# A hybrid decoder layer on one core: fourth quarter copied by ScalarE, branch stages one step later, left sums on GpSimd, scores over 128 rows, spatial products pinned

## The chip, the cores and the metric

The kernel runs on one core of a Trainium2 chip. The metric is the device time of the whole program in microseconds, the median of three runs. A profiled execution of the same program gives the rows of the trace. TensorE has its matmuls (PE) and its weight loads (PEld) in rows of their own; DVE is VectorE, ACT is ScalarE, POOL is GpSimd, SP is SyncE, which here issues most of the DMAs.

## The reference

One decoder layer on 2048 tokens of width 1024. The normalised input is projected once, by a matrix of 9992 columns, into four branches of width 512 and the logits of four gates:

```python
h = _rmsnorm(x, norm_pre)
cols = h @ w_in
y_a = _deltanet_branch(dn_qkv, dn_z, dn_b, dn_a, conv_w, a_log, dt_bias, dn_norm)
y_b = _spatial_gating_branch(gm_uv, gm_z, gm_norm, spatial_w, spatial_b)
y_c = _sliding_window_branch(sw_q, sw_k, sw_v, sw_z, sinks)
y_m = _memory_branch(xm_q, xm_z, mem_kv)
proj = jnp.einsum("btnc,ncd->btnd", ys, w_up)
merged = jnp.sum(gates * proj, axis=2)
return x + _rmsnorm(merged @ w_out, norm_post)
```

Branch A is a gated delta rule in chunks, with a short causal convolution on its inputs and a triangular solve per chunk. Branch B mixes 128 positions per channel group by a causal matrix. Branch C is attention over a window of 128 tokens with 8 query heads on 2 key heads of 64 channels. Branch M attends to 256 memory tokens.

## The kernel before

**Tiling.** The tokens are worked off in four passes of 512 (`TB`). Values are kept in float32 and split into a high and a low part of the matmul type (`hi`, `lo`, lines 234 to 248), so that each product is three matmuls (`mac3`, lines 271 to 273). ScalarE casts the high part of a weight tile (line 243), VectorE or GpSimd subtracts for the low one (line 244).

**Quads.** In the first pass a projection of 256 columns (`proj2`) is done directly, and sums of weight tiles are formed on GpSimd (line 362) and kept in device memory. In the other three passes each projection is a `quad`: a scheme with seven products in place of eight on halves of the 1024 input channels and of the 512 tokens. Its four output quarters C11, C12, C21 and C22 lie in two PSUM banks, C11 and C21 in the first, C12 and C22 in the second. Between the products ScalarE and VectorE copy and add quarters: line 315 copies C11 to C12 after the first product, line 318 keeps C21 as `p7` after the second, lines 321 and 322 add C12 to C21 after the third, and line 324 makes C22 from C12 and `p7` after the fifth. The last two products then end the first and second bank. Two quads run alternately (`job`), one some steps ahead of the other. Each pass has 37 of them. Three of the products take sums and differences of the input's quarters as left factors, which `left_sums` makes at the head of a pass (lines 465 to 484), from the same input tiles that the next `branch_b_v` reads.

**The order of the work.** Everything is written as Python generators. One generator is in the foreground (`fg`); each time that it yields, `step` advances every background generator by one. So a `yield` in a side branch says how many steps of the foreground's products lie before its next instructions in the program text. A scheduler then orders each engine's instructions by a model of their times, near to the text's order but not bound to it; `tc.keep_in_program_order` binds an instruction behind the one that stands before it on its engine. On the chip each engine takes its instructions strictly in the resulting order.

**The places touched.**
- The constants' rows (`crow`, lines 182 to 187) come by DMA from ScalarE's and GpSimd's queues, after the first eight loads of x on SyncE's (line 89).
- `dn_gates` makes the decay logits `g`, waits nine steps, and then does three cumulative products (`gps`, lines 687 to 689).
- `dn_step` solves the triangular systems on VectorE in 32 pairs of instructions (lines 839 and 840) with a scratch tile `pr`, sends the solution through device memory (line 852), waits four steps and goes on with the products of line 862.
- `normalize` (line 943) squares the scan's output on ScalarE one step after the scan made it.
- `mix` in `branch_b` does the four spatial products of a channel group (line 1014), and its output is split (`ysplit`, line 560 on ScalarE) three steps later.
- `branch_c_kv` keeps the keys' high part twice: for each of the two key heads `kph` has the head's 64 channels in its own half of the rows, and a copy in the other half, where the queries hold their low part. The low part `kpl` is one tile, with each head's 64 channels in its own half.
- `block` in `branch_c` does the scores of 128 queries and 256 keys: per pair of query heads and key head one product over all 128 rows (line 1117) and one over the 64 rows of the head with `kpl` (line 1120). A step after the row maxima come the exponentials (line 1138).
- `part` in `branch_m` likewise has exponentials one step behind the maxima (line 1213).

## Time and profile before

| | us |
|---|---|
| median of three runs | 2882.06 |
| lowest and highest | 2878.23, 2888.78 |
| the profiled execution | 2874.15 |
| its span, first to last instruction | 2872.4 |
| TensorE busy | 2683.5 (93%) |
| VectorE busy | 1937.6 (67%) |
| ScalarE busy | 1395.2 (49%) |
| GpSimd busy | 975.8 (34%) |

The busy time of an engine is the union of its instructions' times over the span. A row of the timeline gives start, duration, engine, line, operation, tiles, shape and count, and in brackets the idle time of that engine just before it with what ended it. A row of waits gives an engine's instruction, whom it waited for, the total, how many times, and the longest.

### The profile page before, as it was taken

The page shows a single profiled execution, that of the slowest core. Times are in us where ns is not written, and L with a number is a line of the kernel's source. Part 1 is how long each engine was busy: PE and PEld are TensorE (multiplying, and loading weights), DVE is VectorE, ACT ScalarE, POOL GpSimd, SP SyncE. Part 2 cuts the span into 40 slices and gives each one's busy share as a digit, 9 for nine tenths or more (in the row PEclk, how much of TensorE's full clock was granted, in tenths as well). Part 3 has the DMA queues.
Part 4 walks back from the last instruction along what each step waited for, and adds up shares of the span by engine and source line. Part 5 has one row for each costly group of instructions (what it writes and reads, how often), then busy time and mean ns, then how long its engine had stood idle before and what let it go on. Part 6 is the DMA issues. An engine that isn't in the chain of part 4 may idle for free. (4 is left out here: it accounts for less than half of the span.)

```text
span 2872.4 us, 49476 instructions
## 1 busy us (share of the span) xinstructions
PE 2683.5 (93%) x17457; PEld 2350.7 (82%) x17457; DVE 1937.6 (67%) x3914; ACT 1395.2 (49%) x3116; POOL 975.8 (34%) x848
## 2 busy tenths in 40 slices
PE   7989998999989999999999899999998989998998
PEld 5867777888788888889879888888987988887987
DVE  7576687555676768766568676786556876777654
ACT  4434342433475455355456446545455644644543
POOL 3524444354236443101223634310124363421011
PEclk9999999999999999999999999999999999999999
DMA  5364544455356354445635535444553553553553
GB/s 173 113 182 147 165 136 136 120 167 191 119 136 164 109 132 134 121 114 139 196 99 147 157 98 138 138 119 122 147 180 112 150 148 96 151 142 89 148 151 121
DMA packets 465791, 398.22 MB, mean 139 GB/s; under 512 B 101440, under 2 KB 360584, under 8 KB 465544
## 3 DMA queue, kind: packets, MB, share of 16 engines
q1 hardware_dynamic: 444056, 356.23, 45.0%
q10 hardware_dynamic: 21392, 38.84, 3.7%
q8 instruction: 137, 2.24, 0.3%
q14 instruction: 110, 0.90, 0.1%
q0 software_dynamic: 96, 0.01, 0.0%
HBM read 338.60 MB, written 50.86 MB: 136 GB/s over the span
## 5 line engine op out<-in xcount | busy, mean ns | idle before, releaser
L599 POOL TENSOR_TENSOR merged<-merged,gt 128x512 f32<-128x512 f32 x96 | 141.0, 1471 | 657.4 <-DVE gt L598 630.7
L362 POOL TENSOR_TENSOR T<-raw 128x512 f32<-128x512 f32 x74 | 103.5, 1408 | 98.6 <-DMA raw<-in_w_in_dram 68.4
L839 DVE TENSOR_TENSOR pr<-L,U 128x8 f32<-128x8 f32 (+31 forms) x256 | 111.6, 436 | 23.9 <-DMA L<-scr 18.6
L244 DVE TENSOR_TENSOR gate3lo<-raw,gate3hi 128x512 fp32r<-128x512 f32 x100 | 73.0, 733 | 66.8 <-ACT gate3hi L243 66.0
L244 POOL TENSOR_TENSOR gate1lo<-raw,gate1hi 128x512 fp32r<-128x512 f32 x69 | 88.0, 1290 | 79.0 <-ACT gate1hi L243 65.0
L244 DVE TENSOR_TENSOR gate0lo<-raw,gate0hi 128x512 fp32r<-128x512 f32 x100 | 77.8, 781 | 53.9 <-ACT gate0hi L243 53.2
L243 ACT CAST gate2hi<-raw 128x512 fp32r<-128x512 f32 x100 | 61.8, 621 | 104.8 <-PE gate L272 63.8
L243 ACT CAST gate1hi<-raw 128x512 fp32r<-128x512 f32 x100 | 61.0, 618 | 104.8 <-PE gate L272 45.3
L362 POOL TENSOR_TENSOR T<-raw,T 128x512 f32<-128x512 f32 x74 | 105.4, 1425 | 15.1 <-issue 6.8
L271 PE MATMUL wo<-wohi,mh 128*128 128x512 f32 x256 | 102.6, 401 | 6.3 <-DVE gt L598 6.3
L271 PE MATMUL gate<-hhi,gate1hi 128*128 128x256 f32 (+1 forms) x256 | 86.6, 338 | 20.3 <-DVE gate L322 20.3
L243 ACT CAST gate3hi<-raw 128x512 fp32r<-128x512 f32 x100 | 61.7, 621 | 90.4 <-PE gate L272 46.4
L243 ACT CAST gate0hi<-raw 128x512 fp32r<-128x512 f32 x100 | 62.0, 620 | 85.7 <-PE gate L272 48.2
L273 PE MATMUL wo<-wohi,ml 128*128 128x512 f32 x256 | 100.1, 391 | 0.0
L272 PE MATMUL wo<-wolo,mh 128*128 128x512 f32 x256 | 99.7, 389 | 0.0
L271 PE MATMUL gate<-hhi,gate2hi 128*128 128x256 f32 (+1 forms) x256 | 83.8, 327 | 11.4 <-DVE gate L322 11.4
L244 DVE TENSOR_TENSOR gate2lo<-raw,gate2hi 128x512 fp32r<-128x512 f32 x100 | 73.8, 739 | 27.2 <-ACT gate2hi L243 26.9
L952 POOL TENSOR_TENSOR or<-ov,mhalf 128x2 f32<-128x2 f32 x32 | 23.4, 730 | 190.4 <-DVE ov L950 190.4
L598 DVE SCALAR_TENSOR_TENSOR gt<-gt,up 128x512 f32<-128x512 f32 x96 | 65.0, 681 | 29.1 <-PE up L273 28.5
L273 PE MATMUL gate<-hhi,gate1lo 128*128 128x256 f32 (+1 forms) x256 | 83.8, 330 | 0.4 <-POOL gate1lo L244 0.4
L272 PE MATMUL gate<-hlo,gate1hi 128*128 128x256 f32 (+1 forms) x256 | 83.8, 327 | 0.0
L271 PE MATMUL gate<-hhi,gate0hi 128*128 128x256 f32 (+1 forms) x256 | 80.7, 315 | 2.7 <-ACT u L321 2.1
(644 smaller groups left out, 11036.9 us busy)
## 6 DMA issues: line engine op xcount, KB each, us to landing
raw<-in_w_in_dram SPq DMA_DIRECT2D x461, 256.0 KB, 3.1
raw<-tsum SPq DMA_DIRECT2D x444, 256.0 KB, 2.9
tsum<-T ACTq DMA_DIRECT2D x148, 256.0 KB, 3.7
raw<-in_w_up_dram SPq DMA_DIRECT2D x96, 256.0 KB, 2.9
raw<-in_w_out_dram SPq DMA_DIRECT2D x64, 256.0 KB, 3.1
raw<-in_w_in_dram SPq DMA_DIRECT2D x104, 128.0 KB, 2.9
xx<-in_x_dram SPq DMA_DIRECT2D x32, 256.0 KB, 5.3
raw<-in_w_up_dram SPq DMA_DIRECT2D x64, 128.0 KB, 3.0
```

Source lines behind the costliest of these rows:

```text
L243: A.copy(hi, raw)
L244: ins = eng.tensor_tensor(lo, raw, hi.bitcast(F32), op=ALU.subtract)
L271: ins = T.matmul(ps, lh, rh, start=first, stop=False, skip_group_check=more)
L272: T.matmul(ps, lh, rl, start=False, stop=False, skip_group_check=more)
L273: T.matmul(ps, ll, rh, start=False, stop=last, skip_group_check=more)
L362: G.tensor_tensor(raw[n], raw[u], raw[v], op=ALU.subtract)
L598: V.scalar_tensor_tensor(t, t, 1.0, ps, op0=ALU.add, op1=ALU.mult)
L599: G.tensor_tensor(merged[:, d], merged[:, d], t, op=ALU.add)
L839: V.tensor_tensor(pv, L[:, i, i:32].unsqueeze(1).broadcast_to([P, 8, n]), U[:, :, i:32], op=ALU.mult)
L952: G.tensor_tensor(r, v, mhalf[:, :2], op=ALU.pow)
```

## The change

- The rows of constants are loaded by SyncE, ahead of the rows of x.
- In a quad ScalarE copies C12 to C22 after the fifth product, and VectorE adds `p7` in place.
- All four left sums of a half are made on GpSimd; before, two of them were VectorE's.
- The low part of the keys gets a tile for each key head, with zeros in the other head's rows, cleared by GpSimd at the start of `branch_c_kv`. The score products with it run over all 128 rows, and each follows its high partner at once.
- The cumulative products of the decay gates come after 14 steps in place of nine in the last three passes; the first solve's result is used after eight steps in place of four; the scan's norm, the split of the mixed output, and the exponentials of the window and the memory attention come one step later.
- The first of a group's spatial products is bound to its place in the text.
- The solve's scratch comes from the ring `e` of six buffers, once for the whole solve.

```diff
--- before.py
+++ after.py
@@ -91,2 +91,8 @@
 
+    crow = tmp("crow")[0:69, 0:P]
+    nc.sync.dma_start(crow[0:8], norm_pre[0].rearrange("(k p) -> k p", p=P))
+    nc.sync.dma_start(crow[8:56], conv_w[0].rearrange("j (c p) -> (j c) p", p=P))
+    nc.sync.dma_start(crow[56:64], norm_mem[0].rearrange("(k p) -> k p", p=P))
+    nc.sync.dma_start(crow[64:68], gm_norm[0].rearrange("(k p) -> k p", p=P))
+    nc.sync.dma_start(crow[68:69], dn_norm[0].rearrange("(k p) -> k p", p=P))
     first_rows = [load_rows(x[t * P:(t + 1) * P], "x", dtmp) for t in range(NB)]
@@ -181,8 +187,2 @@
 
-    crow = tmp("crow")[0:69, 0:P]
-    nc.scalar.dma_start(crow[0:8], norm_pre[0].rearrange("(k p) -> k p", p=P))
-    nc.scalar.dma_start(crow[8:56], conv_w[0].rearrange("j (c p) -> (j c) p", p=P))
-    G.dma_start(crow[56:64], norm_mem[0].rearrange("(k p) -> k p", p=P))
-    G.dma_start(crow[64:68], gm_norm[0].rearrange("(k p) -> k p", p=P))
-    G.dma_start(crow[68:69], dn_norm[0].rearrange("(k p) -> k p", p=P))
     ccol = cp.tile([P, 69], F32, name="ccol")
@@ -229,3 +229,3 @@
 
-    nsplit, solving, fast = [0], [], []
+    nsplit, solving, solved, fast = [0], [], [], []
     ON_DVE = ("gu", "gv", "gz", "az", "xq", "xz", "gate0", "gate2", "gate3", "u0", "u2", "u3", "wo")
@@ -323,3 +323,4 @@
             elif i == 4:
-                V.tensor_tensor(ps["C22"], ps["C12"], p7, op=ALU.add)
+                A.copy(ps["C22"], ps["C12"])
+                V.tensor_tensor(ps["C22"], ps["C22"], p7, op=ALU.add)
             elif i >= 5:
@@ -471,3 +472,3 @@
                 a[n] = tmp("s1") if n == "A22" else ctmp("sa")
-                (G if n in ("A22", "A12") else V).tensor_tensor(r3(a[n], 2), h.bitcast(F32)[:, js], l.bitcast(F32)[:, js], op=ALU.add)
+                G.tensor_tensor(r3(a[n], 2), h.bitcast(F32)[:, js], l.bitcast(F32)[:, js], op=ALU.add)
             V.tensor_tensor(a["A22"], a["A21"], a["A22"], op=ALU.add)
@@ -495,3 +496,3 @@
         return (tp.tile([P, 2 * (P + TB)], F32R, name=f"{nm}h", tag="cma", bufs=1),
-                tp.tile([P, H * MEM], F32R, name=f"{nm}l", tag="cmb", bufs=1),
+                tp.tile([P, 2 * (P + TB)], F32R, name=f"{nm}l", tag="cmb", bufs=1),
                 tp.tile([P, 2 * W], F32, name=f"{nm}v", tag="cmv", bufs=1))
@@ -500,3 +501,3 @@
         h, l, v = cm
-        return (h[:, :H * MEM].rearrange("p (h m) -> p h m", h=H), l.rearrange("p (h m) -> p h m", h=H),
+        return (h[:, :H * MEM].rearrange("p (h m) -> p h m", h=H), l[:, :H * MEM].rearrange("p (h m) -> p h m", h=H),
                 v.rearrange("p (a c) -> p a c", a=2))
@@ -682,4 +683,3 @@
                         nexpa.unsqueeze(1).broadcast_to([P, NB, H]), op=ALU.mult)
-        for _ in range(9):
-            yield
+        yield from wait(14 if fast else 9)
         gps = dnp("gps")
@@ -834,5 +834,5 @@
         work = 0
+        pr = etmp("pr")
         for i in range(31, -1, -1):
             n = 32 - i
-            pr = tp.tile([P, 256], F32, name="pr", tag="pr", bufs=1)
             pv = pr[:, :8 * n].rearrange("p (a b) -> p a b", a=8)
@@ -852,3 +852,4 @@
         nc.sync.dma_start(ltv, scu.rearrange("a b j i -> (b j) a i"))
-        yield from wait(4)
+        yield from wait(4 if solved else 8)
+        solved.append(q)
 
@@ -943,3 +944,3 @@
             def normalize(c=c, o=o):
-                yield
+                yield from wait(2)
                 ss = small("oss", 2)
@@ -1013,3 +1014,5 @@
                     for c in range(NB):
-                        T.matmul(sps[:, c * P:(c + 1) * P], vs[c][:, g * P:(g + 1) * P], wsT[:, g], start=True, stop=True)
+                        ins = T.matmul(sps[:, c * P:(c + 1) * P], vs[c][:, g * P:(g + 1) * P], wsT[:, g], start=True, stop=True)
+                        if c == 0:
+                            tc.keep_in_program_order(ins)
                     s = tmp("gs")
@@ -1023,2 +1026,3 @@
                     yield
+                    yield
                     ys.append(ysplit(s, "yb"))
@@ -1032,3 +1036,4 @@
     def branch_c_kv(p):
-        kp2, kpl, vtt = cm_tiles("kp")
+        kp2, kpl2, vtt = cm_tiles("kp")
+        kpl = kpl2.rearrange("p (a b) -> p a b", a=2)
         kph = kp2.rearrange("p (a b) -> p a b", a=2)
@@ -1038,3 +1043,6 @@
             V.tensor_copy(kph[rs, a, 0:P], kch.bitcast(F32)[rs])
-        V.tensor_copy(kpl[:, 0:P], kcl.bitcast(F32))
+        for a in range(2):
+            rs, ro = slice(a * 64, (a + 1) * 64), slice(64 - a * 64, 128 - a * 64)
+            G.tensor_copy(kpl[ro, a], zero[ro].broadcast_to([64, P + TB]))
+            V.tensor_copy(kpl[rs, a, 0:P], kcl.bitcast(F32)[rs])
         V.tensor_copy(vt[:, 0], vc)
@@ -1046,5 +1054,5 @@
                     A.copy(kph[rs, a, P:], ps[rs])
-                    V.tensor_tensor(kpl[rs, P:P + TB], ps[rs], kph.bitcast(F32)[rs, a, P:], op=ALU.subtract)
+                    V.tensor_tensor(kpl[rs, a, P:], ps[rs], kph.bitcast(F32)[rs, a, P:], op=ALU.subtract)
+                    V.tensor_copy(kcl[rs], kpl.bitcast(F32)[rs, a, TB:TB + P])
                     V.tensor_copy(kch[rs], kph.bitcast(F32)[rs, a, TB:TB + P])
-                V.tensor_copy(kcl, kpl.bitcast(F32)[:, TB:TB + P])
 
@@ -1117,5 +1125,3 @@
                     T.matmul(pss[a][:, i * 256:(i + 1) * 256], qs[i][a][:, bs], kph[:, a, kw], start=True, stop=False)
-                for a in range(2):
-                    rs = slice(a * 64, (a + 1) * 64)
-                    T.matmul(pss[a][:, i * 256:(i + 1) * 256], qs[i][a][rs, bs], kpl[rs, kw], start=False, stop=True)
+                    T.matmul(pss[a][:, i * 256:(i + 1) * 256], qs[i][a][:, bs], kpl[:, a, kw], start=False, stop=True)
             for a in range(2):
@@ -1134,3 +1140,3 @@
             V.tensor_tensor(i2(es_), i2(nm), sv, op=ALU.add)
-            yield
+            yield from wait(2)
             den = small("cden", 4)
@@ -1208,3 +1214,3 @@
             V.tensor_scalar_mul(m, m, -1.0)
-            yield
+            yield from wait(2)
             pr = ctmp("xp")
```

## Rows read from the trace of the kernel before

**Rows 1.** The page: busy time of TensorE, share of the span, instructions.

```profile
PE 2683.5 (93%) x17457; PEld 2350.7 (82%) x17457; DVE 1937.6 (67%) x3914; ACT 1395.2 (49%) x3116; POOL 975.8 (34%) x848
```

**Rows 2.** Waits of TensorE over the whole span: total, times, longest.

```profile
PE gate L271 <- DVE gate L322: 32.3, 15, 4.7
...
PE z L862 <- DMA lt<-scu: 14.1, 5, 6.0
...
PE gps L687 <- DVE g L681: 11.7, 3, 3.9
...
PE xq L271 <- ACT u L321: 8.0, 3, 2.7
...
PE xz L271 <- ACT xz L315: 7.6, 3, 2.5
...
PE sq L271 <- ACT sq L315: 7.3, 6, 2.0
...
PE gv L272 <- DVE gvlo L244: 5.2, 4, 1.5
...
PE gs L1014 <- ACT gv L991: 4.5, 6, 1.2
```

**Rows 3.** Timeline of TensorE: one block of scores, first pass.

```profile
248.45 0.39 PE L1117 MATMUL scp<-kph,sq 128*128 128x256 f32 x2
...
248.78 0.38 PE L1120 MATMUL scp<-kpl,sq 64*128 64x256 f32 x2
...
249.83 0.50 PE L271 MATMUL gate<-hhi,gate1hi 128*128 128x512 f32 x1
```

**Rows 4.** Timeline of TensorE: full products of 256 columns, one behind another.

```profile
1400.00 0.28 PE L272 MATMUL gate<-hlo,gate0hi 128*128 128x256 f32 x1
...
1400.12 0.28 PE L273 MATMUL gate<-hhi,gate0lo 128*128 128x256 f32 x1
```

**Rows 5.** Timeline of ScalarE, third pass: a split and the copy behind it.

```profile
1602.27 0.62 ACT L560 CAST ybh<-gs 128x512 fp32r<-128x512 f32 x1 [3.71 <-DVE gs L1022]
...
1603.32 0.36 ACT L315 COPY sq<-sq 128x256 f32<-128x256 f32 x1
```

**Rows 6.** Timeline of ScalarE, second pass: the tanh and the copy behind it.

```profile
1106.46 0.63 ACT L713 ACTIVATE dnvt<-dnva 128x512 f32<-128x512 f32 x1 [0.60 <-DVE dnva L708]
...
1107.18 0.36 ACT L315 COPY xz<-xz 128x256 f32<-128x256 f32 x1
```

**Rows 7.** Timeline of ScalarE, third pass: the square in the scan's norm.

```profile
1945.63 0.31 ACT L947 ACTIVATE junk<-on 128x128 bf16<-128x128 f32 x1 [2.37 <-DVE on L941]
```

**Rows 8.** Windows: busy time of each engine in ten microseconds, granted clock.

```profile
1500.00:1510.00 10.00, 7.01 (x31) 6.75 (x32) 3.12 (x17) 7.71 (x16) 2.92 (x4) 0.52 0.14 39
```

**Rows 9.** Timeline of TensorE, second pass: second product of a quad.

```profile
1353.71 0.39 PE L271 MATMUL gate<-shi,gate0hi 128*128 128x256 f32 x1 [0.43 <-ACT gate L315]
```

**Rows 10.** Timeline at the head of the third pass: TensorE and ScalarE.

```profile
1505.46 1.22 PE L1014 MATMUL gs<-wsT,gv 128*128 128x128 f32 x4 [0.30 <-ACT gv L991]
...
1505.93 0.36 ACT L315 COPY dn<-dn 128x256 f32<-128x256 f32 x1
...
1506.34 0.56 PE L271 MATMUL dn<-hhi,dn1hi 128*128 128x256 f32 x1
```

**Rows 11.** Timeline of the start: SyncE's loads of x, TensorE.

```profile
0.81 3.74 SPq L89 DMA_DIRECT2D xx<-in_x_dram  x8
...
12.53 0.35 PE L190 MATMUL cps<-ident,crow 69*128 69x69 f32 x1 [7.00 <-DMA crow<-in_conv_w_dram]
...
18.49 2.64 PE L444 MATMUL xtp<-ident,xx 128*128 128x128 f32 x13 [2.13 <-DVE xx L430]
```

**Rows 12.** Timeline at the end of the second pass: VectorE and GpSimd.

```profile
1474.00 1.74 POOL L472 TENSOR_TENSOR sa<-hhi,hlo 128x512 f32<-128x512 f32 x1 [0.27 <-DVE slo L481]
...
1474.50 1.79 DVE L481 TENSOR_TENSOR slo<-sa,shi 128x512 fp32r<-128x512 f32 x1
...
1476.87 1.28 DVE L472 TENSOR_TENSOR sa<-hhi,hlo 128x512 f32<-128x512 f32 x2
```

## The prediction, made before the changed kernel was run

> **What bounds the kernel now.** I read the page's busy times first. TensorE is busy 93% of the span [rows 1], so the time is TensorE's own work plus its idle 7%, about 189 us (2872.4 less 2683.5). A helper engine matters only where TensorE stands for it, or where its work is laid on TensorE. I then read TensorE's waits: they are short and many [rows 2]. VectorE and ScalarE end nearly all of them, and most rows count a multiple of three, because the last three passes repeat one schedule. Last I read timelines around those waits, to see what stood ahead of the late instruction on its own engine. Engines take their queues in order, so a late instruction delays everything behind it. That view decides what "one step later" is worth, since the edit moves an instruction back in a queue and takes no work away.
>
> **Scores at 128 rows.** A block now has four 128-row and four 64-row products of 256 columns, in alternating pairs. The eight take from 248.45 to 249.83, 1.38 us [rows 3]; 22 of the 32 blocks lie within 1.3 to 1.5 us. Products of the same columns on 128 rows throughout start 0.12 us apart [rows 4], so eight would take 0.96. The 64-row pairs thus cost more than full ones, 0.42 us a block, 13.4 us in 32 blocks. A few blocks stand beside waits that keep part of it, so I take **-12**. The Trainium skill (TensorEngine Tiling, Theoretical Speedup) says that a contraction of 64 lets two row tiles run at once, up to twice as fast. By it a pair costs one slot, six slots 0.72 us, and the change loses 0.24 us a block. The same page (Key Properties) says that a change of tiling mode drains the engine; the 1.38 us side with that sentence and against the first.
>
> **Stages one step later.** Three waits per pass have one form: ScalarE stands at an instruction of a side branch, and a copy out of a quarter product (lines 315, 318, 321) that TensorE needs is queued behind it.
> - The split of a gated output stands 3.71 us for VectorE, and the copy for the query projection comes only behind it [rows 5]. TensorE's share is 2.0 us, the longest of its sq row [rows 2], once a pass: 6.0 us.
> - The softmax exponentials and the convolution's tanh stand ahead of the xz copy [rows 6]: 7.6 us in three passes [rows 2].
> - The square of the scan's output stands 2.37 us for VectorE [rows 7], ahead of the copies for xq: 8.0 us [rows 2].
>
> Together 21.6 us. A step later, the copy can go first. I don't take all of it. In the second case the tanh itself had stood 0.60 us for VectorE, and with the exponentials gone it may hold the copy to the same time. In all three the next late thing is a VectorE sum or a weight split. I take half, **-11**, between 0 and -21.6. The clock adds to any such gain. Where TensorE stood long its granted clock fell afterwards: 0.52 in ten microseconds of which it was busy seven [rows 8], near its lower level of 1.2 GHz. I leave that for the range.
>
> **Decay gates five steps later, spatial products pinned.** At the head of each of the last three passes TensorE's queue holds products for the spatial branch that wait for ScalarE (4.5 us) and the cumulative sums that wait for VectorE (11.7 us) [rows 2]. Both edits take these out of the way, 16.2 us if that were the end. It need not be. The second product of the first quad writes the bank which the copy of line 315 reads, and such a product waits for that copy even where nothing else is in the way [rows 9]. Here the copy runs at 1505.93, behind ScalarE's GELUs, squares and scalings, and TensorE resumes at 1506.34 [rows 10]. Unless ScalarE's order changes, the hole stays, and the spatial products leave it for places where TensorE is busy: at 1.2 us or less for four of their records [rows 10], some 2 us a pass. I take **-3**, between -16 and +6.
>
> **First solve.** Its result waits 6.0 us for the DMA that brings the solution back [rows 2]; four more steps of other work cover that, and nothing before the next gate of the pass needs the scan. Only the first solve changes, as its list is never emptied. **-6**.
>
> **Constants by SyncE.** TensorE no longer stands 7.0 us for them, but it then stands for the rows of x anyway and resumes at 18.49 for the last of these [rows 11]. Eight loads take 3.74 us to issue, so five more ahead put the rows 2.3 us later. ScalarE's queue saves two issues, GpSimd's three. **+2**, between -3 and +4.
>
> **Left sums on GpSimd.** Twelve sums of 0.64 us (two in 1.28) leave VectorE, 7.7 us; GpSimd's own sum there takes 1.74. They lie in the stretch in which VectorE is full and TensorE ends up waiting for a split (5.2 us in four waits) [rows 2, 12]. Against it stands the row in which a GpSimd sum runs and a VectorE split beside it takes 1.79 us, where such an instruction takes 0.64 alone [rows 12]: 1.15 us for each of twelve is 14. The Trainium skill (GPSIMD Engine Reference, the SBUF interfaces) says that GpSimd contends with VectorE instructions that have two SBUF inputs, and this row agrees. GpSimd's roots for the last output and splits queue behind the sums too. I take **0**, between -5 and +14.
>
> **Fourth quarter by ScalarE.** The copy comes once a quad, 37 quads a pass by the calls, 111 in all, at 0.36 us [rows 5]: 40 us more on ScalarE, and the VectorE addition stays at its length. Nobody waits for that addition now. The new chain is longer, copy then addition, before the last product writes the same bank. It is covered by the fifth product and, where two quads alternate, by the other quad's products of 12 x 0.12 = 1.44 us each. What costs is a copy that stands in ScalarE's queue ahead of a weight cast or another copy. Bounds: 0 if covered; the sister chain at the third quarter, with a cover of one product less, costs TensorE 32.3 us for the addition and 8.0 for the copy [rows 2], so +40. With the longer cover I take **+4**.
>
> **The rest.** Two GpSimd clears a pass, two small VectorE copies in place of one, and the solve's scratch taken from a ring of six shared buffers. No row shows such a clear; each lies between a short GpSimd instruction and the 1.7 us sum of [rows 12]. Eight of them at most stretch VectorE by 1.15 us: 0 to +9. Scores need the cleared half only several quads later. I take **+1**. The later step of the memory branch's exponentials and the wait in the scan's norm change no total.
>
> **The sum** is -12 -11 -3 -6 +2 +0 +4 +1 = -25. The profiled execution took 2874.15 us, of which the span is 2872.4, so 2849. The median shown is 7.9 us above that execution; I add it: **2857 us**.
>
> **The rivals.**
> - *Everything comes home.* All waits aimed at vanish and no cost shows: -13.4 -21.6 -16.2 -6 -5, -62, and 2820. For it: each edit has a wait of its size. Against: ScalarE's own chain at the head of a pass, and the queues behind each wait. 0.12.
> - *The waits change their name.* The steps and pins gain nothing, as the next instruction in line is as late: -12 -6 +7 = -11, so 2871. For it: VectorE is full in the very stretches where these waits stand. 0.22.
> - *ScalarE becomes the bound, and the kernel slower.* The copies cost the +40 of the sister chain, and the one-step gains, which are ScalarE's own time, are gone: -12 -3 -6 +2 +40 +1 = +22, so 2904. It decides once the copy starts more than the cover, some 2.9 us, after its product. For it: ScalarE stands that long in [rows 5]. Against: half of ScalarE's time is free, and no wait for the present addition is seen. 0.09.
> - *A pair of 64-row products is one slot after all*, the 1.38 us having another cause: +7.7 in place of -12, so 2877. The 0.12 us spacing of full products speaks against it. It is what the Trainium skill's first sentence above would give. 0.03.
>
> **How the numbers follow.** My forecast has 0.54, its own range 2838 to 2872 by the bounds of the steps and sums. Half a percent, 14.4 us, is about what a measurement of this kernel can tell from no change: faster is below 2867.7, slower above 2896.5. Faster holds most of the forecast (0.47), the first rival (0.12) and a third of the second (0.07): 0.66. Slower is the third rival, 0.09. The rest is 0.25. From 2824 to 2886 leaves out the outer part of the first rival and the third.
>
> **What the profile after would show.** Blocks of scores at 0.96 us, 128-row products alone. No TensorE wait for the cumulative sums, nor for copies of line 315 behind a split of an output. The hole at the head of a later pass either still ends at line 315's copy, as I say, or is gone. A wait of the last product of a quad for the added copy or the addition behind it would show the third rival. A longer VectorE split beside GpSimd's sums, with a longer TensorE wait at the end of the gv product, would show the price of the left sums. I am wrong if TensorE's idle falls by much more or less than some 14 us.

## The result, and the profile after

The changed kernel takes **2901.4 us** (median of 13 runs, 2896.0 to 2912.9), the kernel before in the same comparison 2885.8 (2877.0 to 2891.8). The ratio is 1.0065, 95% interval 1.005 to 1.008: slower by 0.65%, some 19 us, where -25 was forecast and the range ended at 2886. In this section and the next a difference in microseconds is the ratio less one, times the median of before in that comparison; the interval is worked out likewise. A profiled execution is one execution, and can lie more than 10 us from its kernel's median, as here: it took 2912.4 us, with a span of 2910.7.

The busy times of the page after, engines in the order of [rows 1]:

```profile
PE 2685.3 (92%) x17457; PEld 2362.4 (81%) x17457; DVE 1930.4 (66%) x3910; ACT 1424.4 (49%) x3227; POOL 995.1 (34%) x865
```

TensorE is as busy as before (2685.3 against 2683.5) and idle for 225 us in place of 189. The rows of TensorE's waits in the changed kernel that answer to [rows 2], or are new or larger beside it (engine, line, whom it waited for, total us, times, longest):

```profile
PE gate L271 <- DVE gate L322: 26.5, 13, 4.7
PE gps L687 <- DVE g L682: 17.0, 3, 5.8
PE z L863 <- DMA lt<-scu: 14.7, 2, 7.9
PE scp L1125 <- DVE szs L1167: 10.1, 7, 3.1
PE gate L271 <- DVE gate L325: 9.2, 6, 1.8
PE gv L272 <- DVE gvlo L244: 9.2, 6, 2.2
PE xq L271 <- ACT u L321: 9.0, 3, 3.0
PE xz L271 <- ACT xz L315: 8.3, 3, 2.8
PE scp L1125 <- DMA sq<-sqlo: 8.0, 5, 2.8
...
PE sq L271 <- ACT sq L315: 7.3, 6, 2.0
PE up L273 <- DVE u2lo L244: 7.0, 9, 1.3
```

The reader is to see three things. The waits at which the steps were aimed are all there: sq for line 315 7.3 us as before, xz for line 315 8.3 (7.6), xq for line 321 9.0 (8.0), gps for g 17.0 (11.7), z for its DMA 14.7 (14.1). Only gs for gv has gone. And four have come or grown by 6 us or more: the gate product for line 325, which is the addition behind the new copy (9.2, none before), up for the split of u2 (7.0, none before), the score product for line 1167, the window's output (10.1, in before 2.6 on its line 1161), and the score product for the load of the query's split (8.0, in before 2.0).

What did come as forecast is the score block, first pass, TensorE's timeline (start, duration, engine, line, operation, tiles, shape):

```profile
252.99 0.36 PE L1125 MATMUL scp<-kph,sq 128*128 128x256 f32 x1
253.19 0.28 PE L1126 MATMUL scp<-kpl,sq 128*128 128x256 f32 x1
253.30 0.28 PE L1125 MATMUL scp<-kph,sq 128*128 128x256 f32 x1
...
254.02 0.40 PE L271 MATMUL gate<-hhi,gate1hi 128*128 128x512 f32 x1
```

From 252.99 to 254.02 it takes 1.03 us for eight products, against 1.38 in [rows 3]; over 32 blocks the products take some 11 us less. The kernel loses some 30 us elsewhere.

### The profile page after: what moved, and what is told of

Read it like the earlier page. It is cut to its first block, busy times and chain, and to the rows that moved or that the text cites. A ratio compares the mean times of both kernels' runs of the same rounds, so it can differ in the third digit from the quotient of the medians.

```text
span 2910.7 us, 49597 instructions
## 1 busy us (share of the span) xinstructions
PE 2685.3 (92%) x17457; PEld 2362.4 (81%) x17457; DVE 1930.4 (66%) x3910; ACT 1424.4 (49%) x3227; POOL 995.1 (34%) x865
## 5 line engine op out<-in xcount | busy, mean ns | idle before, releaser
L839 DVE TENSOR_TENSOR pr<-L,U 128x8 f32<-128x8 f32 (+31 forms) x256 | 114.7, 448 | 21.2 <-DMA L<-scr 15.3
L244 DVE TENSOR_TENSOR gate0lo<-raw,gate0hi 128x512 fp32r<-128x512 f32 x100 | 78.8, 793 | 55.6 <-ACT gate0hi L243 55.5
L1149 POOL TENSOR_TENSOR sc<-sc,cden 128x512 f32<-128x512 f32 x32 | 41.3, 1292 | 153.8 <-DVE cden L1148 106.7
L271 PE MATMUL gate<-hhi,gate3hi 128*128 128x256 f32 (+1 forms) x256 | 84.2, 329 | 0.2
```

The source lines that it names most:

```text
L244: ins = eng.tensor_tensor(lo, raw, hi.bitcast(F32), op=ALU.subtract)
L271: ins = T.matmul(ps, lh, rh, start=first, stop=False, skip_group_check=more)
L839: V.tensor_tensor(pv, L[:, i, i:32].unsqueeze(1).broadcast_to([P, 8, n]), U[:, :, i:32], op=ALU.mult)
L1149: G.tensor_tensor(scv, scv, den.unsqueeze(2).broadcast_to([P, 4, P]), op=ALU.mult)
```

## The experiments

Each kernel below is the kernel before with the edits named, unless it says otherwise. "The other steps" are the first solve, the norm, the output split and the gates.

| kernel | edits | difference, us | 95% |
|---|---|---|---|
| a_scores | scores on 128 rows | -9.5 | -14.1 to -4.6 |
| b_exps | both exponentials later | +12.7 | +7.2 to +18.1 |
| m_expw | the window's exponentials later | +12.7 | +8.1 to +17.3 |
| n_expm | the memory branch's later | +1.7 | -2.9 to +6.3 |
| c_copy | fourth copy by ScalarE | +0.6 | -4.9 to +6.3 |
| d_left | left sums on GpSimd | +7.5 | +2.6 to +12.4 |
| e_rest | the other steps | -8.7 | -14.4 to -2.6 |
| f_pin | pins and gates | +2.0 | -2.3 to +6.3 |
| g_crow | constants by SyncE | -1.2 | -6.6 to +4.3 |
| i_scrc | scores, other steps, constants | -6.9 | -10.9 to -2.9 |
| j_copy | i_scrc and the fourth copy | -1.4 | -6.0 to +3.2 |
| l_pin | i_scrc and the pins | -8.4 | -13.0 to -3.5 |
| h_part | i_scrc, the copy and the pins | -4.0 | -8.4 to +0.6 |
| s_noexpw | changed kernel, window's exponentials as before | +10.7 | +6.0 to +15.6 |
| r_noleft | changed kernel, left sums as before | +17.3 | +11.8 to +22.8 |
| k_bound | output split later, and bound | -6.0 | -12.4 to 0 |
| o_scbound | scores, and that split | -12.7 | -17.8 to -7.5 |
| p_setbound | i_scrc, and that split | **-20.7** | -26.5 to -15.3 |

**The scores alone.**

```diff
-                for a in range(2):
-                    rs = slice(a * 64, (a + 1) * 64)
-                    T.matmul(pss[a][:, i * 256:(i + 1) * 256], qs[i][a][rs, bs], kpl[rs, kw], start=False, stop=True)
+                    T.matmul(pss[a][:, i * 256:(i + 1) * 256], qs[i][a][:, bs], kpl[:, a, kw], start=False, stop=True)
```

> Only the scores on 128 rows (with the two GpSimd clears, the wider buffer and the ring for the solve's scratch). Theory A, the parts of the prediction hold and add: 11 to 13 us faster than before, since the blocks of the changed kernel already measure 0.95 to 1.04 us in place of 1.38. Theory B, the gain in a block is given back at waits of TensorE for VectorE that end at the same time as before, because VectorE has the same work: within 4 us of before, score blocks at 0.96 us all the same, and TensorE's idle larger by what its busy time lost. In the changed kernel TensorE's wait of the scores for the split of the query grew from 2.0 to 8.0 us and that for line 1167's product from 2.6 to 10.1; under B both grow here too, under A neither does.

Ratio 0.9967: -9.5 us, nearer to theory A, with an interval that ends just beyond B's 4 us. TensorE's busy time fell to 2671.7, 11.8 less than before, and neither of the two waits that B named grew: the score products stand 1.5 us for the load of the query's split (2.0 before) and 1.0 for the window's output (2.6). So these two waits of the changed kernel belong to other edits. B's other sign did come: TensorE's idle in this profile is 202.2 us, 13.3 more than before, in many small waits of other products. So a part of the gain may be given back, and -9.5 is not the gain of the blocks alone.

**The later exponentials.**

```diff
-            yield
+            yield from wait(2)
             den = small("cden", 4)
...
-            yield
+            yield from wait(2)
             pr = ctmp("xp")
```

> Only the two later steps of the exponentials (window and memory branch), the one pair of the moved steps that changes much of the order in which the engines' queues are filled. Theory A: no time of its own to 5 us faster, the wait of the xz product for line 315's copy (7.6 us before) shorter. Theory B, a later step moves the branch's other instructions, and what they wait for is as late as ever, in another place: slower by 3 to 12 us, with the xz wait at 7 to 9 us and a longer wait for the first solve or for the memory branch's products.

+12.7, above B's range. The wait of xz for line 315 is 7.5 us: the step didn't take it away. The up product's wait for the split of u2 (6.8 us, nine times) is the changed kernel's. The two edits were then taken apart.

> Only the window's exponentials two steps later. Theory A, these carry the cost of the pair, as they are what reorders more of TensorE's queue and of VectorE's (the window's products of all four quads of a gate): +9 to +14 us, with the up product's wait for its weight split (6.8 us in nine, none before) and the memory branch's products' waits. Theory B, the memory branch's carry it: within 4 us of before.

> Only the memory branch's exponentials two steps later. Theory A, the window's carry the cost: within 4 us of before. Theory B: +9 to +14 us. Under both the wait of the xz product for line 315 stays at 7 to 8 us, since on ScalarE's queue that copy still stands behind the same tanh and casts.

The window's step costs it all, +12.7, the memory branch's +1.7. But m_expw's profile shows that most of this is neither of the waits expected. The score products' groups on TensorE, before and then m_expw (line, shape, count, busy us, mean ns, idle ahead of them):

```profile
L1117 PE MATMUL scp<-kph,sq 128*128 128x256 f32 x128 | 30.8, 313 | 5.3 <-DVE szs L1161 2.6 <-DMA sq<-sqlo 2.0 <-ACT dn L315 0.7
L1120 PE MATMUL scp<-kpl,sq 64*128 64x256 f32 x128 | 24.8, 384 | 0.0
```

```profile
L1117 PE MATMUL scp<-kph,sq 128*128 128x256 f32 x128 | 38.7, 339 | 5.8 <-DVE szs L1161 3.5 <-DMA sq<-sqlo 2.3
L1120 PE MATMUL scp<-kpl,sq 64*128 64x256 f32 x128 | 37.3, 386 | 0.0
```

The 64-row products are busy 37.3 us in place of 24.8, the 128-row ones 38.7 in place of 30.8, with little change of the means. The two groups overlap each other; counted once, TensorE is busy with score products for 66.2 us in place of 49.1, 17 more. One such product isn't longer, but fewer of them overlap. TensorE's timeline of half a block, and its weight loads in the same stretch:

```profile
277.73 0.39 PE L1117 MATMUL scp<-kph,sq 128*128 128x256 f32 x1
278.05 0.38 PE L1120 MATMUL scp<-kpl,sq 64*128 64x256 f32 x1
278.36 0.38 PE L1117 MATMUL scp<-kph,sq 128*128 128x256 f32 x1
278.67 0.38 PE L1120 MATMUL scp<-kpl,sq 64*128 64x256 f32 x1
278.98 0.50 PE L271 MATMUL gate<-hhi,gate1hi 128*128 128x512 f32 x1
```

```profile
278.05 0.18 PEld L1120 LDWEIGHTS scp<-kpl,sq 64*128 64x128 f32 x1
278.36 0.19 PEld L1117 LDWEIGHTS scp<-kph,sq 128*128 128x128 f32 x1
```

In before, TensorE has all 64-row products in pairs, 64 of them, and the two of a pair run at once: a pair takes 0.38 us in [rows 3], and so does the single product here. The later step made the scheduler deal half of them out singly: 32 pairs and 64 singles. Then 64 and 128 rows alternate at every product, each weight load begins only with its own product (278.05 in both), and products start 0.31 us apart. In the changed kernel, where all have 128 rows, they start 0.12 apart, and the load runs ahead: that of the product at 253.19 above is

```profile
253.07 0.19 PEld L1126 LDWEIGHTS scp<-kpl,sq 128*128 128x128 f32 x1
```

So the 12.7 us here is mostly a cost that the scores on 128 rows take away, and can't be added up beside them.

**The copy and the left sums.**

```diff
-                V.tensor_tensor(ps["C22"], ps["C12"], p7, op=ALU.add)
+                A.copy(ps["C22"], ps["C12"])
+                V.tensor_tensor(ps["C22"], ps["C22"], p7, op=ALU.add)
```

> Only the fourth quarter's copy by ScalarE, with VectorE's addition behind it. Theory A, the longer chain is covered: +4 us and no wait on the new addition. Theory B, the third rival on a smaller scale: the waits of the gate product for the new addition that the changed kernel shows (9.2 us in six, none before) come back here, with some more at copies and weight casts that stand behind the new copy on ScalarE: +9 to +20 us.

+0.6, with theory A's +4 inside the interval. TensorE waits for the new addition nowhere in this kernel, so the 9.2 us of the changed kernel need another edit beside the copy. What came with the copy is the score products' wait for the load of the query's split: 6.4 us, 2.0 before and 8.0 in the changed kernel.

```diff
-                (G if n in ("A22", "A12") else V).tensor_tensor(r3(a[n], 2), h.bitcast(F32)[:, js], l.bitcast(F32)[:, js], op=ALU.add)
+                G.tensor_tensor(r3(a[n], 2), h.bitcast(F32)[:, js], l.bitcast(F32)[:, js], op=ALU.add)
```

> Only the left sums on GpSimd. The order of TensorE's and ScalarE's queues is that of before, so this is the clean price of the move. Theory A: 0, with the wait at the end of the gv product (5.2 us in four) no longer than before. Theory B, GpSimd's sums take longer and lie in front of what TensorE needs, or lengthen VectorE's splits beside them: the gv wait at 8 to 10 us, as in the changed kernel (9.2), and +3 to +14 us.

+7.5, theory B, with a wait of gv for its split of 9.9 us. GpSimd's and VectorE's timelines at the head of the third pass:

```profile
1483.25 1.74 POOL L472 TENSOR_TENSOR sa<-hhi,hlo 128x512 f32<-128x512 f32 x1 [0.34 <-DVE finv L416]
...
1485.92 1.43 POOL L472 TENSOR_TENSOR sa<-hhi,hlo 128x512 f32<-128x512 f32 x1
```

```profile
1482.49 0.68 DVE L481 TENSOR_TENSOR slo<-sa,shi 128x512 fp32r<-128x512 f32 x1
...
1483.76 1.78 DVE L481 TENSOR_TENSOR slo<-sa,shi 128x512 fp32r<-128x512 f32 x1
...
1486.13 1.77 DVE L481 TENSOR_TENSOR slo<-sa,shi 128x512 fp32r<-128x512 f32 x1
```

It is the pattern of [rows 12]. Beside a sum on GpSimd a VectorE split takes 1.78 and 1.77 us, the same split with no such sum beside it 0.68. In the last three passes seven splits and additions of `left_sums` are stretched like this, against two before. So VectorE is rid of 7.7 us of sums, and gets some 5.5 back in longer instructions ahead of the split that TensorE waits for. That this makes the 7.5 us isn't shown. The wait of gv grew by 4.7 us, but other waits are shorter: TensorE's idle in this profile is 186.2 us, in before's 188.9.

**The other steps, the pins, the constants.**

```diff
-        yield from wait(4)
+        yield from wait(4 if solved else 8)
+        solved.append(q)
...
             def normalize(c=c, o=o):
-                yield
+                yield from wait(2)
...
                     yield
+                    yield
                     ys.append(ysplit(s, "yb"))
...
-        for _ in range(9):
-            yield
+        yield from wait(14 if fast else 9)
```

> Only the other moved steps: first solve, norm, output split, gates (the exponentials stay where they were). In the built kernel TensorE's products stand almost in the order of before, and those of the first solve (z) stand at the same place, behind the last product of skv. Theory A, the steps of the prediction hold: 6 us for the first solve and a few for the norm, so -6 to -12. Theory B, the scheduler puts an instruction by its model of the times, not where the text has it, so a later yield moves next to nothing: within 4 us of before, the first solve still waiting 5 to 7 us for its DMA and the waits for line 315 in front of sq (7.3) and for g (11.7) unchanged.

-8.7, on A's side, but for none of A's reasons. The first solve's product stands 6.33 us for its DMA, xq 7.4 behind the norm's square (8.0 before), sq 7.4 for line 315, gps 11.7 for g. In the built programs the gates' edit alone leaves the order of all engines as it was, and the split's alone moves one VectorE instruction in each of three passes; the first solve's products stand behind the last skv product as before. What did change is the order behind them, and with the norm's edit that of some two dozen products. Which of the changed places gives the 8.7 us wasn't separated; this profile can't tell, as its execution took 13.5 us more than the kernel's median.

```diff
+                        if c == 0:
+                            tc.keep_in_program_order(ins)
```

> Only the pinned spatial products and the later gates. Theory A, the prediction: -3, with the products' own waits (gs for gv, 4.5 us) gone from the table of waits and the hole at the head of a pass ending with line 315's copy as before. Theory B: the hole in front of the cumulative sums (gps for g) takes over their time, 11.7 us before and 17.0 in the changed kernel, and the whole stays within 3 us of before. Theory C: pinned products pull TensorE behind the later ones, +4 to +8.

+2.0, no difference beyond the interval: theory B. The head of the third pass on TensorE:

```profile
1507.45 0.58 PE L686 MATMUL gps<-g,triu 128*128 128x16 f32 x2 [5.84 <-DVE g L681]
...
1511.11 0.58 PE L271 MATMUL dn<-shi,dn0hi 128*128 128x256 f32 x1 [1.61 <-ACT dn L315]
```

gs has left the hole, gps stands there for 5.84 us in place of 3.9, and the second product of the quad then stands for line 315, as forecast; 17.5 and 4.8 us over the span, where gs for gv had 4.5 and gps 11.7.

```diff
-    nc.scalar.dma_start(crow[0:8], norm_pre[0].rearrange("(k p) -> k p", p=P))
+    nc.sync.dma_start(crow[0:8], norm_pre[0].rearrange("(k p) -> k p", p=P))
```

(and its four fellows, all ahead of the rows of x)

> Only the constants' rows by SyncE, ahead of the rows of x. Theory A, the prediction: +2 (-3 to +4), the 7.0 us wait for crow gone, but the rows of x later. Theory B, from the changed kernel's trace, where TensorE's steady stream begins at 15.67 us in place of 18.49: 1 to 3 us faster.

-1.2, in either theory's range. The wait for the constants fell from 7.0 to 3.8 us, and TensorE's steady stream begins at 15.97 us in place of 18.49.

**Sets of edits.** The sum of the parts measured alone, -9.5 +12.7 +0.6 +7.5 -8.7 +2.0 -1.2, is +3.4. The changed kernel has +18.8. With seven intervals of about 5 us to either side, the sum is known to some 14 us only.

> The changed kernel without the later exponentials and with the left sums where they were before. Theory A, the parts add: 19 us of the changed kernel's own excess over before, less 12.7 us that the exponentials alone cost and 7.5 that the left sums alone cost, so about 2 to 4 us below before. Theory B, each set of edits draws another order of the queues, so that the parts don't add: more than 8 us off that number, to either side.

> Scores on 128 rows, the later first solve, norm, output split and gates, and the constants by SyncE; no later exponentials, no fourth copy, no pins, left sums as before. Theory A, parts that each paid by themselves add: -9.5 (scores), -8.6 (the other steps), -1.2 (constants) = -19 us against before, about 2865. Theory B, they overlap, the scheduler drawing a new order for the set, as the set with copy and pins came to -4 where its parts sum to -17: within 6 us of before.

> The same set with the fourth quarter's copy by ScalarE. Theory A, the copy costs what it cost alone, under 2 us: as the set without it. Theory B, beside the other edits the copy is what costs the 13 us by which the larger set missed the sum of its parts: 8 to 15 us over the set without it, with the waits for sq's load or for line 315 copies longer.

> The same set with the pinned spatial products instead of the copy. Theory A, pins cost what they cost alone: +2 us over the set without them. Theory B, the pins carry the 13 us: 8 to 15 over it, with the wait of the cumulative sums at 17.5 us in place of 11.7 and the second-product wait of dn for line 315 (4.8 us, none in before) the larger part.

h_part came to -4.0, where theory A's subtraction put it. But that was luck of the sums: the parts of which it consists have -16.8 alone. i_scrc should have some -19 by its theory A and has -6.9, nearer to B, though the intervals of three parts together are wide. The copy adds 5.5 us to i_scrc by the medians, between its two theories, though the intervals overlap, with the wait for the load of the query's split again at 7.0 us; the pins add nothing, their theory A.

> The changed kernel with the window's exponentials where they were before. Theory A, what they cost alone was the 64-row products standing singly, so beside scores of 128 rows they cost little: +14 to +19 over before, as the changed kernel. Theory B, their new order of the queues has waits of its own in the changed kernel: the up product's for its split (7.0 us), the gate product's for the addition behind the new copy (9.2, 1.8 in the set without these edits), the scores' for line 1167's product (10.1, 3.5): 10 to 18 us below the changed kernel, with these three under 6 us together.

+10.7, so the window's step costs 8.1 us in the changed kernel by the medians, some 2 to 15 by the two intervals: just short of theory B. Its waits are B's. Two of the three named are, in s_noexpw:

```profile
PE scp L1125 <- DVE szs L1167: 3.5, 2, 3.2
...
PE gate L271 <- DVE gate L325: 1.8, 3, 0.6
```

The split of u2 is not waited for at all; the three are 5.3 us together, against 26.3 in the changed kernel. How the copy and the window's step together make the wait for the addition longer (9.2 us; 1.8 in s_noexpw, and 3.3 in m_expw, which has no copy) is seen in the second pass of the changed kernel; ScalarE, VectorE and TensorE in turn:

```profile
1225.59 0.37 ACT L324 COPY gate<-gate 128x256 f32<-128x256 f32 x1
```

```profile
1226.07 1.78 DVE L858 STREAM_TRANSPOSE inv<-lt 32x256 f32<-32x256 f32 x4 [3.51 <-DMA lt<-scu]
1227.89 0.69 DVE L244 TENSOR_TENSOR xqlo<-raw,xqhi 128x512 fp32r<-128x512 f32 x1
1228.50 0.42 DVE L325 TENSOR_TENSOR gate<-gate,p 128x256 f32<-128x256 f32 x1
```

```profile
1228.98 0.57 PE L271 MATMUL gate<-shi,gate2hi 128*128 128x256 f32 x1 [1.77 <-DVE gate L325]
```

ScalarE's copy is done at 1225.96. VectorE's addition starts only at 1228.50, as the solve's transposes, which had waited 3.51 us for the DMA of the solution, and a weight split stand ahead of it in VectorE's queue. TensorE stands 1.77 us for it, the longest of the six. In s_noexpw the same transposes start at 1212.33, with no wait ahead of them.

> The changed kernel with the left sums where they were before; TensorE's and ScalarE's queues are those of the changed kernel. Theory A, the left sums cost beside the other edits what they cost alone: 7.5 us below the changed kernel's +19, so +11, with TensorE's wait of gv for its split back from 9.2 to about 5 us. Theory B, they cost nothing more here, the waits of the new order being the longer ones: within 3 us of the changed kernel.

+17.3 against +18.8: theory B by the time, though the wait of gv for its split fell to 4.6 us as in A. Beside the other edits the left sums cost 1.5 us by the medians, nothing that intervals of 5 us to either side can tell from 0.

**A step that does move.**

```diff
-        A.copy(h, y)
+        ins = A.copy(h, y)
+        if name == "yb":
+            tc.keep_in_program_order(ins)
...
                     yield
+                    yield
                     ys.append(ysplit(s, "yb"))
```

> Only the output split one step later, but with ScalarE's part of it bound to its place in the program text, so that the scheduler can't bring it forward again: in the built kernel TensorE's queue is that of before, and on ScalarE the split now stands behind the copy of line 315 for which the first query product waited 2.0 us once a pass. Theory A, the prediction's reason was right and only the edit failed to move the instruction: TensorE's wait of sq for line 315 falls from 7.3 us to 1 to 3, and the kernel is 3 to 6 us faster. Theory B, the copy was held by something else, or the next product waits as long: the wait stays over 5 us, or another grows by as much, and the time stays within 3 us of before.

ScalarE's timeline in the place of [rows 5], the changed kernel and then k_bound:

```profile
1628.38 0.62 ACT L561 CAST ybh<-gs 128x512 fp32r<-128x512 f32 x1 [3.46 <-DVE gs L1025]
...
1629.42 0.36 ACT L315 COPY sq<-sq 128x256 f32<-128x256 f32 x1
```

```profile
1604.64 0.37 ACT L315 COPY sq<-sq 128x256 f32<-128x256 f32 x1
...
1612.20 0.65 ACT L560 CAST ybh<-gs 128x512 fp32r<-128x512 f32 x1
```

In the changed kernel the split still stands ahead of the copy, waiting 3.46 us for VectorE. Bound, it stands 7.6 us behind it. TensorE's wait of sq for line 315 fell from 7.3 to 1.3 us, and the kernel is 6.0 us faster, with an interval that just reaches 0: theory A.

> Scores on 128 rows and the bound output split, nothing else. TensorE's queue is that of the scores alone. Theory A, the two gains add: -9.5 and -6, so some 15 us below before, 2866. Theory B, the gain of the split is taken back by the next wait: as the scores alone, 9 to 10 us below before, with the sq wait for line 315 under 2 us all the same.

> Scores, later first solve, norm and gates, constants by SyncE, and the output split bound. Theory A, the bound split adds its 6 us to what this set gave without it (-6.9): -13. Theory B, the set's own new order has other waits as long, within 3 us of the set without the binding.

Scores and the bound split: -12.7, between the two theories. With the other steps and the constants: -20.7, ratio 0.9928 (0.9908 to 0.9947), 2858.3 us. It is the fastest kernel here. Its set without the binding had -6.9, so by the medians the binding is worth 13.8 in it and 6.0 alone; the intervals are too wide to tell these apart.

## Why the prediction was wrong

**The step that failed** is "the edit moves an instruction back in a queue". It moves it in the text, and a scheduler of its own orders each queue. The section on the kernel says so, and the prediction didn't use it. Of the moved steps the gates' and the split's move next to nothing; the first solve's leaves its products where they were; the norm's moves more, but the wait behind its square stays at 7.4 us for 8.0; the exponentials' moves much, but the wait of the xz copy stays at 7.5 us for 7.6. So the terms -11 for the steps and -6 for the first solve had no ground in the edit. That the reason behind them was sound is shown for one of the three waits: bound to its place the split does let the copy go first, and 6.0 us of sq's wait go, the size that was forecast for it.

**A cost that the sum had not.** A step that does reorder brings waits of its own. The steps' term ran from 0 to -21.6, so that a later step had no price at all. By the runs the window's step alone costs 12.7 us, mostly in 64-row products that stand singly, and 8.1 of the changed kernel's 18.8, where such products are gone and TensorE and VectorE have another order of work with other waits. The sum took the edits as terms that add, each with a gain or a price at its own place, and this price belongs to no place. The range was made of the bounds of terms, and held no term for it.

**The fourth copy.** The cover was looked for on TensorE and the price on ScalarE. It came on VectorE, whose addition had been early enough before. Alone it is +0.6, inside the bounds and below the +4, in i_scrc +5.5; beside the window's step there is the wait on "the addition behind it" that the third rival was to show, 9.2 us, not 40.

**The left sums.** The sum took 0 from the range of -5 to +14. Alone it is +7.5. The mechanism of the upper end is in the trace, but at seven instructions in place of twelve, and that it makes the time is not shown; r_noleft shows that the left sums aren't what makes the changed kernel slow. The Trainium skill (GPSIMD Engine Reference, the SBUF interfaces) agrees here too, with 1.78 against 0.68 us.

**What held.** The scores: -9.5 alone, for -12, and blocks of 1.03 us for 0.96. The rival by which a pair of 64-row products is one slot gave a loss of 7.7, and has fallen by its time. Its premise has not: the two products of a pair do run at once, which the reading of [rows 3] passed over. What a block of 1.38 us pays for is the change between 64 and 128 rows, as the singles of m_expw show. The pins: the hole at the head of the pass still ends at line 315's copy, and +2.0 lies in the range of -16 to +6. The constants: -1.2 in the range. The rival that the waits would change their name was the nearest in kind, but gave 2871: the new waits are longer than the old.

**The clock** was left to the range. TensorE's busy time times the granted clock's shortfall, summed over slices of 10 us, is 71.9 us in the changed kernel's profile and 55.6 in before's. The mean granted clock of single executions tells more. In 136 executions of the kernel before that were measured beside the experiments it lies between 0.964 and 0.978, 0.971 on average, and the time falls by some 1.8 us for each 0.001 that the clock is higher. The changed kernel's 13 executions average 0.968. An estimate by that slope, at equal clock, leaves it some 16 us slower than those 136: the clock is the smaller part of its loss. The same estimate moves other rows of the table. s_noexpw, at 0.967, comes to +4, so that the window's step would cost some 12 us in the changed kernel; d_left (0.969) comes to +4, a_scores (0.974) to -5, e_rest to -5, k_bound to -5, p_setbound to -22; i_scrc comes to -9, where its three parts sum to -8, and the seven parts alone sum to some +16. So the +3.4 beside the +18.8 doesn't by itself show that the edits don't add; what shows it is the window's step, whose price alone stands in 64-row products which the changed kernel hasn't got. Equally, what h_part and i_scrc lack against their parts may be the clock's. Whether an edit lowers the clock, or its few executions happened to get a lower one, stays open.

Open as well: what of the 14.7 us between h_part and s_noexpw is the left sums', what the memory branch's later step (7.5 and 1.7 alone) and what the clock's, and which place gives e_rest its gain.

## What to carry to other kernels

Where a scheduler orders the queues, compare the built order on each engine before any edit of the text is given a price; an edit that changes no queue has none, and one that reorders a queue is judged whole, not by the wait that it aimed at. Move an instruction by binding it, and change one thing at a time: the version with the steps that paid and the bound split is 0.7% faster, while the full set is 0.65% slower. A price found beside another arrangement (the exponentials beside 64-row scores) can't be carried over to one where its cause is gone. And where differences are below 1%, compare the granted clocks of the executions before a difference is given to an edit.

## What the runs showed of the hardware

Two products on 64 rows each, on different halves of the rows, run at once: 0.38 us for the pair in [rows 3], 0.38 for one in m_expw. What costs is the change between 64 and 128 rows. Where it comes at every product, products start 0.31 us apart in place of 0.12, and the weight load, which elsewhere runs ahead of its product, begins only with it; which of the two sets the 0.31 isn't separated. In alternating pairs eight took 1.38 us, on 128 rows throughout 1.03. The Trainium skill (TensorEngine Tiling, Key Properties) has a drain at a change of tiling mode, and the 0.31 us agree. The speedup for the small contraction (the Trainium skill, TensorEngine Tiling, Theoretical Speedup) shows inside a pair, and the changes around it cost more than it gives.

A GpSimd sum of two tiles stretches a VectorE split beside it from 0.68 to 1.78 us. With all left sums on GpSimd this comes at seven of VectorE's splits and additions there, in before at two.
